# The output gate's low-rank products in three passes of split operands

## The chip, the core and the metric

The kernel runs on one core of a Trainium2 chip. The metric is device time in microseconds of one execution. Five engines work side by side, each through its own list of instructions in order: TensorE (PE in the profile, its weight loads PEld), VectorE (DVE), ScalarE (ACT), GpSimd (POOL) and SyncE (SP). They wait for each other by semaphores. Matmul results land in PSUM, everything else lives in SBUF, and the weights come from memory by DMA.

## The reference

One layer of an encoder trunk, 256 tokens, model width 2048, all in float32. The input is normalised, one combined projection feeds three mixers, their outputs are gated and summed, then an output projection, a norm, and an MLP with squared ReLU. The first mixer is stick-breaking attention, the second forgetting attention, the third an RWKV-7 time mix with 16 heads of 64. The change lies in the third:

```python
r, k, v, wd, ad, gd = _split(z, (RWKV_WIDTH,) * 3 + (DECAY_LORA, AAA_LORA, GATE_LORA))
w_log = -jax.nn.softplus(-(w0 + jnp.tanh(wd) @ w_up)) - 0.5
a = jax.nn.sigmoid(a0 + ad @ a_up)
g = jax.nn.sigmoid(gd) @ g_up
...
y = ((y - mean) * lax.rsqrt(var + RWKV_GN_EPS) * ln_w + ln_b)
y = y + jnp.sum(r_h * k_h * r_k, axis=-1, keepdims=True) * v_h
return y.reshape(b, s, RWKV_WIDTH) * g
```

`g` is the output gate: 160 inner channels (`GATE_LORA`), a sigmoid, and a product with `g_up`, 160 by 1024. The 160 channels are laid out as 128 and 32. The result `y * g` is the operand of the third branch, `y_c @ w_branch_c`.

## The kernel before

**The main stream.** The weights come as one stream of halves of 128 x 1024 floats. `wraw` loads a half on SP's queue, `wsplit` cuts it into a rounded part (`whi`, an ACT copy, line 173) and a rest (`wlo`, a DVE subtraction, line 175); each of `raw`, `whi` and `wlo` has three buffers. The activations are cut the same way: 16 tiles `pk` of 512 columns, 256 of the rounded part and 256 of the rest. A product is then three passes of rounded operands (high times high, high times low, low times high), on type float32r. `unit` (lines 191, 195, 197) gives a tile of channels by tokens; `tok` (lines 220, 235) gives tokens by 512 channels, with 12 matmuls of 512 columns per weight half. In `tok`, the last half runs first for the first 128 tokens and then for the other 128 (line 220). `gate` is one `tok` of eight halves with a tanh as evacuation (line 1017), `branch` one `tok` over a mixer's output (four halves for the third mixer), with two DVE operations as evacuation (lines 1029, 1030).

**The mixers.** All three are one Python generator, `mixers()`, whose steps are emitted between the matmuls of the main stream. `tick(f)` adds 0.88 f to a credit, at most up to 1.5, and takes f from a hold; while the credit is positive and the hold has run out, `step()` emits the next piece, and the piece's own cost, written in its `yield`, is taken from the credit. A yield of `("stage", cost, hold)` sets a hold as well and ends the tick. A yield of `("need", key)` stops until the main stream has produced that tile. `tok` ticks with 0.7, 0.5 and 0.5 per half, with 1.0 twice in the last half; `unit` ticks with 1.0 twice per half. Each `branch` takes 0.6 or 1.2 per 128 tokens from the credit.

TensorE's order is the order of emission, by hand. In this part of the kernel ACT, DVE, POOL and the queues are ordered by the planner, which takes an instruction once its operands and buffers are free, in favour of those emitted earlier.

**The third mixer.** `rwkv_lora` (lines 655 to 663) applies tanh and sigmoid to the low-rank inputs: `xl` for decay and learning rate, which is split into `xs` for rounded products, and `sy` (128 channels of the gate) and `zz` (the gate's other 32 on partitions 0 to 31, copied onto 32 to 63 by line 660), which stay plain fp32. Then `rwkv_half` runs twice, for eight heads each: key norms (L709 to L717), four gate steps (`gates`, with rounded products on line 731 in two row groups), the triangular inverse in the buffer `Ti` (L819 to L867), four chunks of the state (right-hand sides in the buffer `rh`, read by line 885), and at last two blocks of group norm, each for two pairs of heads:

- the gate weights `gq` are loaded by four DMAs on ACT's queue (lines 924, 925), into a buffer of their own, `gup`;
- squares, and their split into `hi`, `lo` (lines 929 to 932), then a stage with cost 0.1 and hold 2.5;
- sums over heads in two passes (lines 100, 101), the gate products in plain fp32 (lines 938 and 941, the latter on 32 partitions, one pair of heads per row group);
- variance, power by Ln and Exp with their table loads (lines 942, 265, 267), a Newton step (272 to 275), scaling, bias, bonus and gate (950 to 953).

After that `cut` (called at each tick) splits the finished `y` into `pk` tiles for the third branch (lines 256, 257).

**The place in the stream.** The second half's blocks fall into the three third-mixer gates, `thc`, which stand ahead of the third branch. After them the line `while not fin[0]: step()` emits at once what is left of the mixer, and the third branch follows; its operands of the last two pairs of heads are used by its fourth weight half.

Of the kernel before, what the change touches and what calls it, by code (L numbers as in the profile page):

```python
# [11 lines left out]
F32 = mybir.dt.float32  # L12
F32R = mybir.dt.float32r
AF = mybir.ActivationFunctionType
ALU = mybir.AluOpType
# [3 lines left out]
T = 256  # L19
# [33 lines left out]
def hybrid_block(ctx, tc, xt, x, gains, params, consts, lora, gup, wst, out):  # L53
    nc = tc.nc
    V, A, G, PE = nc.vector, nc.scalar, nc.gpsimd, nc.tensor
# [10 lines left out]
    def nm(s):  # L66
        uid[0] += 1
        return f"{s}_{uid[0]}"
# [4 lines left out]
    def mps():  # L73
        return pm.tile([128, 512], F32, tag="mps", name=nm("mps"), bufs=4)
# [4 lines left out]
    def tmp(n=T):  # L79
        return tpool.tile([128, T], F32, tag="tmp", name=nm("tmp"), bufs=3)  # L80
# [22 lines left out]
    def P(name, i=0, r=slice(0, 128)):  # L103
        return par[r, PC[name] + i:PC[name] + i + 1]


    done = {}
# [92 lines left out]
    def unit(pks):  # L200

        ps = gps()
        for h in range(2):
            hi, lo = wnext()
            gemm(ps, hi, lo, pks[8 * h:8 * h + 8], h == 0, h == 1, tick)
        return ps
# [40 lines left out]
    def evac(ps, dst):  # L247
        b = tmp()
        ins = A.activation(b, ps[:, T:2 * T], AF.Copy)
        V.tensor_tensor(dst, ps[:, 0:T], b, ALU.add)  # L250
        return ins
# [11 lines left out]
    def power(y, m, t):  # L263

        A.activation(t, m, AF.Ln)
        yield
        A.activation(y, t, AF.Exp, scale=-0.5)
        yield

    def newton(y, m, t):  # L270

        V.tensor_tensor(t, y, y, ALU.mult)
        V.tensor_tensor(t, t, m, ALU.mult)
        V.tensor_scalar(t, t, -0.5, 1.5, ALU.mult, ALU.add)
        V.tensor_tensor(y, y, t, ALU.mult)

    p1 = ExitStack()
    rp = p1.enter_context(tc.tile_pool(name="rp", bufs=1))
# [3 lines left out]
    def g1(w=T):  # L282
        return rp.tile([128, T], F32, tag="g1", name=nm("g1"), bufs=21)


    z = tmp()
# [353 lines left out]
    def shift(ps, i, dst, n=128):  # L640

        b, t = tmp(), tmp()
        zp = rp.tile([128, T + 1], F32, tag="zp", name=nm("zp"), bufs=2)
        G.memset(zp[:, 0:1], 0.0)
        A.activation(b[0:n], ps[0:n, T:2 * T], AF.Copy)
        V.tensor_tensor(t[0:n], ps[0:n, 0:T], b[0:n], ALU.add)
        A.activation(zp[0:n, 1:T + 1], t[0:n], AF.Copy, scale=P("mu", i, slice(0, n)))
        V.scalar_tensor_tensor(dst, t[0:n], omu[0:n, i:i + 1], zp[0:n, 0:T], ALU.mult, ALU.add)
# [3 lines left out]
    def rwkv_lora():  # L652
        yield ("need", "lora")
        xl, sy, zz = done["zx"], done["zy"], done["zz"]
        A.activation(xl[0:64], xl[0:64], AF.Tanh)
        sz = zz[0:32]
        for s in (sy, sz):
            A.activation(s, s, AF.Tanh, scale=0.5)
            V.tensor_scalar(s, s, 0.5, 0.5, ALU.mult, ALU.add)
        A.activation(zz[32:64], sz, AF.Copy)  # L660
        xs = rp.tile([128, 2, T], F32R, name="xs")
        A.activation(xs[:, 0, :], xl, AF.Copy)
        V.tensor_tensor(xs[:, 1, :], xl, xs[:, 0, :].bitcast(F32), ALU.subtract)
        done["xl"], done["sy"], done["sz"] = xs, sy, zz
        yield 1.5

    def pair(tag="AX", bufs=5):
        return rp.tile([128, 2, T], F32R, tag=tag, name=nm("hl"), bufs=bufs)

    def heads(ps, hi, lo):  # L670
        twice(ps, CR("bones"), *(t.rearrange("p a b -> p (a b)") for t in (hi, lo)))

    def rwkv_half(hf):
        PR = range(4 * hf, 4 * hf + 4)
        xl, sy, sz = done["xl"], done["sy"], done["sz"]
# [10 lines left out]
        for i2 in range(2):  # L686
            hi, lo = pair(), pair()
            for i, p in enumerate(PR[2 * i2:2 * i2 + 2]):
                yield ("need", f"k{p}")
                kx[p] = done[f"k{p}"]  # L690
                s = tmp()
# [81 lines left out]
        for i, p in enumerate(PR):  # L773
# [7 lines left out]
            for cc in range(4):  # L781
                for h in range(2):
                    hr = slice(64 * h, 64 * h + 64)
                    PE.matmul(pss[h][:, cc * 128:cc * 128 + 128], At[p][hr, cc, :], Bt[p][hr, cc, :],
                              start=True, stop=True)
# [30 lines left out]
        Ti = rp.tile([64, 32, 32], F32, tag="Ti", name=nm("Ti"), bufs=1)  # L816
# [9 lines left out]
        for s in range(31):  # L826
            n, m = 31 - s, s + 1
# [37 lines left out]
        for c in range(4):  # L865
# [8 lines left out]
            for i, p in enumerate(PR):  # L874
                for h, hc in enumerate(HC):
                    PE.matmul(psr[hc, co[i]], SC[64:128, sls[i][h], 0:64], Xt[p][64:128, c, hc],
                              start=c == 0 and i == 0, stop=True, skip_group_check=True)
# [26 lines left out]
            for i, p in enumerate(PR):  # L904
                for h, hc in enumerate(HC):
                    PE.matmul(psy[hc, co[i]], Xt[p][:, c, hc], SC[:, sls[i][h], 64:128],
                              start=c == 0 and i == 0, stop=True, skip_group_check=True)
            if c < 3:
                for hr in HC:
                    d, n = psp[hr, 0:T].rearrange("p (a b) -> p a b", a=4), Pb[hr, :, hr]  # L910
# [6 lines left out]
            yield ("stage", 1.5, 1.7)  # L917

        for i2 in range(2):
            gq = rp.tile([128, 3, 128], F32, tag="gup", name=nm("gup"), bufs=1)  # L920
            for i in range(2):
                cs = slice(128 * PR[2 * i2 + i], 128 * PR[2 * i2 + i] + 128)
                with tc.issue_after(behind[1].ins):
                    nc.scalar.dma_start(out=gq[:, i, :], in_=gup[0:128, cs])
                    nc.scalar.dma_start(out=gq[32 * i:32 * i + 32, 2, :], in_=gup[128:160, cs])
            B6 = rp.tile([128, 6, T], F32, tag="b6", name=nm("gn"), bufs=1)
            var, ri, sc = B6[:, 0:2, :], B6[:, 2:4, :], B6[:, 4:6, :]
            for i in range(2):
                A.activation(sc[:, i, :], y[PR[2 * i2 + i]], AF.Square)
            hi, lo = pair(), pair()  # L930
            A.activation(hi, sc, AF.Copy)
            V.tensor_tensor(lo, sc, hi.bitcast(F32), ALU.subtract)
            yield ("stage", 0.1, 2.5)
            ps = mps()
            heads(ps, hi, lo)
            psg = [mps(), mps()]
            for i in range(2):
                PE.matmul(psg[i][:, 0:T], gq[:, i, :], sy, start=True, stop=False)
            for i in range(2):
                r = slice(32 * i, 32 * i + 32)  # L940
                PE.matmul(psg[i][:, 0:T], gq[r, 2, :], sz[r], start=False, stop=True)
            A.activation(var, ps.rearrange("p (a b) -> p a b", a=2), AF.Identity, scale=1.0 / 64, bias=cst[:, 1:2])
            yield ("stage", 0.1, 0)
            for _ in power(ri, var, sc):
                yield ("stage", 0.1, 1)
            newton(ri, var, sc)
            yield 2.2
            for i in range(2):
                p = PR[2 * i2 + i]
                V.tensor_tensor(y[p], y[p], ri[:, i, :], ALU.mult)  # L950
                A.activation(y[p], y[p], AF.Identity, scale=P("lnw", p), bias=P("lnb", p))
                V.tensor_tensor(y[p], y[p], bon[p], ALU.add)
                V.tensor_tensor(y[p], psg[i][:, 0:T], y[p], ALU.mult)
                yc[p] = y[p]
                yield 1.1

    def mixers():
        yield from sb_mix()
        yield from fox_mix()
        yield from rwkv_lora()  # L960
        for hf in range(2):
            yield from rwkv_half(hf)
# [4 lines left out]
    def vtok(sb):  # L967
        vs = []
        for tt, ps in enumerate(tok(xpk if sb else upk)):
            v = rp.tile([128, 512], F32, tag="BK", name=nm("vtok"), bufs=8)  # L970
            if sb:
                A.activation(v, ps, AF.Copy, scale=col[:, 4 * tt:4 * tt + 1])
            else:
                A.activation(v, ps, AF.Copy)
            vs.append(v)
        return vs

    for br in ("sb", "fox"):
        for s in ("q", "k"):
            if br == "sb":  # L980
                continue
            lst = []
            for h in range(4):
                ps = unit(upk)
                t = g1()
                evac(ps, t)
                lst.append(t)
            done[br + s] = lst
        done[br + "v"] = vtok(br == "sb")
        done[br] = True  # L990
        for i, nme, n in ((0, "zx", 128), (1, "zy", 128)) if br == "fox" else ((2, "zz", 36),):
            ps = unit(upk)
            z = rp.tile([128, T], F32, tag="tha", name=nme, bufs=1) if i == 0 else \
                rp.tile([64 if n == 36 else n, T], F32, name=nme)
            shift(ps, MU_X + i, z[0:n], n)
            done[nme] = z
    done["lora"] = True
# [180 lines left out]
    for g in range(4):  # L1178
        gs = slice(512 * g, 512 * g + 512)
# [338 lines left out]
    for g in range(4):  # L1518
        gs = slice(512 * g, 512 * g + 512)
# [140 lines left out]
```

## Time and profile before

| | us |
|---|---|
| median of three runs | 1508.16 |
| lowest, highest | 1507.34, 1508.66 |
| the profiled execution's own time | 1509.36 |
| its span | 1507.6 |

The profile gives one execution. A group is a line, an engine, an operation and its tiles, with durations in ns. The chain of waits is followed back from the last instruction; its pieces have start, length, engine, line and count. In a timeline, a row has start, length, engine, line, operation, output and input, and in brackets the idle time before it and what ended it. A plain fp32 product of 256 columns shows as two TensorE records, a float32r product as one. Matmul ends are modelled, so rows of successive matmuls overlap; the distance of their starts is what TensorE spends on them.

### The profile page before, as it was taken

To read this page: it belongs to the slowest core of one execution; us is meant where nothing else is said; L and a number is where in the kernel's file an instruction comes from. 1 tells how busy PE (TensorE), PEld (TensorE's weight loads), DVE (VectorE), ACT (ScalarE), POOL (GpSimd) and SP (SyncE) were. 2 spreads that over 40 slices of the span, in tenths; PEclk is the share of its full clock that TensorE was granted. 3 is DMA by queue.
4 is the path that set the end of the run, shared out by engine and by line. 5 is a ranking of instruction groups with operands and counts; after the bars stand their busy time and mean duration, and the time that the engine had idled before them with its cause. 6 is when DMAs were issued, how large, how long until landed. Compare 5 with 4: busy or idle time off the path is not lost.

```text
span 1507.6 us, 22703 instructions
## 1 busy us (share of the span) xinstructions
PE 1492.0 (99%) x8384; PEld 1254.0 (83%) x8384; DVE 1206.6 (80%) x1673; ACT 939.8 (62%) x1433; POOL 94.5 (6%) x151
## 2 busy tenths in 40 slices
PE   9999999999999999999999999999999999999997
PEld 7888888887788887788888988888888888888886
DVE  7875679895678796476557778998899989999996
ACT  7665677545676445564545766776667666767663
POOL 0021003000001000000000000000000000000000
PEclk9999999999999999999999999999999999999999
DMA  7655454454455465456675768888888888989874
GB/s 263 197 168 184 142 182 154 154 182 163 156 165 177 154 192 186 130 169 196 231 238 159 265 177 254 229 242 273 263 259 258 244 254 248 258 254 258 246 224 152
DMA packets 104687, 312.71 MB, mean 207 GB/s; under 512 B 10240, under 2 KB 12288, under 8 KB 104576
## 3 DMA queue, kind: packets, MB, share of 16 engines
q1 hardware_dynamic: 93968, 279.87, 56.2%
q0 software_dynamic: 8064, 29.36, 10.5%
q10 hardware_dynamic: 2544, 2.03, 0.5%
q8 instruction: 66, 1.08, 0.3%
q14 instruction: 45, 0.37, 0.1%
HBM read 279.77 MB, written 2.10 MB: 187 GB/s over the span
## 4 chain that ended last, share of the span: by engine, by line
PE 89%; DMA 4%; DVE 2%; issue 2%; ACT 2%; POOLq 0%; SPq 0%; DVEq 0%; POOL 0%; ACTq 0%
PE gps L235 27%; PE gps L191 21%; PE gps L195 12%; PE gps L220 7%; PE mps L1378 3%; PE mps L1380 3%; PE mps L1379 3%; DMA raw<-in_wst_dram 2%; PE gps L1380 2%; PE gps L1378 2%; PE gps L1379 2%; DMA raw<-raw 2%; PE gps L197 1%; DVE wlo L175 1%; ACT whi L173 1%
## 5 line engine op out<-in xcount | busy, mean ns | idle before, releaser
L175 DVE TENSOR_TENSOR wlo<-raw,whi 128x1024 fp32r<-128x1024 f32 x576 | 699.0, 1224 | 159.2 <-ACT whi L173 147.3
L173 ACT ACTIVATE whi<-raw 128x1024 fp32r<-128x1024 f32 x576 | 604.1, 1057 | 260.4 <-PE gps L235 76.3
L191 PE MATMUL gps<-pk,whi 128*128 128x512 f32 x1479 | 375.6, 392 | 1.8 <-DVE tmp L1296 1.0
L191 PEld LDWEIGHTS gps<-pk,whi 128*128 128x128 f32 x1479 | 274.2, 188 | 57.9 <-ACT whi L173 2.3
L235 PE MATMUL gps<-whi,pk 128*128 128x512 f32 x1004 | 253.6, 393 | 0.0
L195 PEld LDWEIGHTS gps<-pk,wlo 128*128 128x128 f32 x1582 | 215.6, 190 | 15.6 <-DVE wlo L175 0.7
L195 PE MATMUL gps<-pk,wlo 128*128 128x256 f32 x1582 | 221.1, 283 | 0.1
L235 PEld LDWEIGHTS gps<-whi,pk 128*128 128x128 f32 x1004 | 186.6, 188 | 39.8 <-issue 1.0
L235 PE MATMUL gps<-wlo,pk 128*128 128x512 f32 x502 | 138.2, 393 | 0.1
L235 PEld LDWEIGHTS gps<-wlo,pk 128*128 128x128 f32 x502 | 93.2, 188 | 20.0 <-DVE wlo L175 0.5
L1378 PE MATMUL mps<-whi,fm 128*128 128x512 f32 x224 | 88.8, 396 | 0.8 <-ACT whi L173 0.6
L1295 ACT ACTIVATE tmp<-gps 128x256 f32<-128x256 f32 x64 | 24.6, 384 | 101.4 <-PE gps L197 99.5
L1379 PE MATMUL mps<-whi,fm 128*128 128x512 f32 x224 | 87.8, 392 | 0.0
L1380 PE MATMUL mps<-wlo,fm 128*128 128x512 f32 x224 | 87.6, 391 | 0.0
L1358 POOL DMA_DIRECT2D raw<-raw x56 | 48.8, 872 | 573.1 <-DVE raw L1355 279.5
L1355 DVE TENSOR_TENSOR raw<-raw,raw 128x1024 f32<-128x1024 f32 x56 | 68.5, 1222 | 0.8
L1378 PE MATMUL gps<-whi,fm 128*128 128x512 f32 x168 | 65.9, 392 | 0.0
L1380 PE MATMUL gps<-wlo,fm 128*128 128x512 f32 x168 | 65.9, 392 | 0.0
L1379 PE MATMUL gps<-whi,fm 128*128 128x512 f32 x168 | 65.5, 390 | 0.0
L220 PE MATMUL gps<-whi,pk 128*128 128x512 f32 x224 | 60.8, 393 | 0.0
L1380 PEld LDWEIGHTS mps<-wlo,fm 128*128 128x128 f32 x224 | 42.1, 188 | 9.7 <-DVE wlo L175 0.2
L1378 PEld LDWEIGHTS mps<-whi,fm 128*128 128x128 f32 x224 | 42.4, 189 | 8.9 <-ACT whi L173 2.9
(346 smaller groups left out, 1726.6 us busy)
## 6 DMA issues: line engine op xcount, KB each, us to landing
raw<-in_wst_dram SPq DMA_DIRECT2D x516, 512.0 KB, 4.4
raw<-raw POOLq DMA_DIRECT2D x56, 512.0 KB, 6.8
x<-in_xt_dram SPq DMA_DIRECT2D x8, 256.0 KB, 6.7
x<-in_x_dram SPq DMA_DIRECT2D x8, 256.0 KB, 4.7
raw<-in_wst_dram SPq DMA_DIRECT2D x4, 256.0 KB, 4.9
g<-in_gains_dram SPq DMA_DIRECT2D x4, 256.0 KB, 4.8
pk<-in_gains_dram SPq DMA_DIRECT2D x4, 256.0 KB, 6.9
out_dram<-x SPq DMA_DIRECT2D x4, 256.0 KB, 2.8
```

Source lines behind the costliest of these rows:

```text
L173: A.activation(hi, raw, AF.Copy)
L175: low = lambda: V.tensor_tensor(lo, raw, hi.bitcast(F32), ALU.subtract)
L191: PE.matmul(ps, hi[:, i * 128:i * 128 + 128], pks[i], start=first and i == 0, stop=False)
L195: PE.matmul(ps[:, 0:T], lo[:, i * 128:i * 128 + 128], pks[i][:, 0:T], start=False, stop=False)
L220: PE.matmul(ps[tt], pks[k][:, c:c + 128], w[:, (k - k0) * 512:(k - k0) * 512 + 512], start=k == 0 and part == 0 and w is hl[0], stop=w is ...
L235: PE.matmul(ps[tt], pks[k][:, c:c + 128], w[:, (k - k0) * 512:(k - k0) * 512 + 512], start=k == 0 and part == 0 and w is hl[0], stop=False)
L1295: A.activation(b, ps[:, T:2 * T], AF.Copy)
L1355: V.tensor_tensor(R[d, a], R[d, a], R[d, b], ALU.add)
L1358: G.dma_start(out=R[d, a], in_=R[d, b], accum_op=ALU.add)
L1378: PE.matmul(Q[f], a, w, start=d == d0 and i == 0, stop=False)
L1379: PE.matmul(Q[f], b, w, start=False, stop=False)
L1380: PE.matmul(Q[f], a, wl, start=False, stop=d == dn and i == 1)
```

## The change

`rwkv_lora` splits the sigmoids `sy` and `zz` into a rounded part and a rest, and its cost goes from 1.5 to 2.5. Each group norm block splits its gate weights too, into `gs`, after a new yield of 0.8, and its stage costs 0.8 in place of 0.1. The gate products are three float32r passes (high by high, high by low, low by high) for each former fp32 product; the passes on 32 partitions alternate between the two row groups. `gq` moves from `gup` into the buffer tag `rh`, `gs` goes into `Ti`, and the projected inputs `zy` and `zz` move from tiles of their own into the tags `em` and `kkr`.

```diff
@@ -658,11 +658,17 @@
         A.activation(zz[32:64], sz, AF.Copy)
+        parts = []
+        for s, n in ((sy, 128), (zz, 64)):
+            t = rp.tile([128, 2, T], F32R, name=nm("ss"))[0:n]
+            A.activation(t[:, 0, :], s[0:n], AF.Copy)
+            V.tensor_tensor(t[:, 1, :], s[0:n], t[:, 0, :].bitcast(F32), ALU.subtract)
+            parts.append(t)
         xs = rp.tile([128, 2, T], F32R, name="xs")
         A.activation(xs[:, 0, :], xl, AF.Copy)
         V.tensor_tensor(xs[:, 1, :], xl, xs[:, 0, :].bitcast(F32), ALU.subtract)
-        done["xl"], done["sy"], done["sz"] = xs, sy, zz
-        yield 1.5
+        done["xl"], done["sy"], done["sz"] = xs, *parts
+        yield 2.5
@@ -917,7 +923,8 @@
         for i2 in range(2):
-            gq = rp.tile([128, 3, 128], F32, tag="gup", name=nm("gup"), bufs=1)
+            gq = rp.tile([128, 3, 128], F32, tag="rh", name=nm("gup"), bufs=1)
+            gs = rp.tile([128, 2, 3, 128], F32R, tag="Ti", name=nm("gs"), bufs=1)
@@ -930,15 +937,22 @@
             V.tensor_tensor(lo, sc, hi.bitcast(F32), ALU.subtract)
-            yield ("stage", 0.1, 2.5)
+            yield 0.8
+            for r, c in ((slice(0, 128), slice(0, 2)), (slice(0, 64), slice(2, 3))):
+                A.activation(gs[r, 0, c, :], gq[r, c, :], AF.Copy)
+                V.tensor_tensor(gs[r, 1, c, :], gq[r, c, :], gs[r, 0, c, :].bitcast(F32), ALU.subtract)
+            yield ("stage", 0.8, 2.5)
             ps = mps()
             heads(ps, hi, lo)
             psg = [mps(), mps()]
+            three = ((0, 0), (0, 1), (1, 0))
             for i in range(2):
-                PE.matmul(psg[i][:, 0:T], gq[:, i, :], sy, start=True, stop=False)
-            for i in range(2):
-                r = slice(32 * i, 32 * i + 32)
-                PE.matmul(psg[i][:, 0:T], gq[r, 2, :], sz[r], start=False, stop=True)
+                for a, b in three:
+                    PE.matmul(psg[i][:, 0:T], gs[:, a, i, :], sy[:, b, :], start=a + b == 0, stop=False)
+            for a, b in three:
+                for i in range(2):
+                    r = slice(32 * i, 32 * i + 32)
+                    PE.matmul(psg[i][:, 0:T], gs[r, a, 2, :], sz[r, b, :], start=False, stop=a == 1)
@@ -990,8 +1004,7 @@
-            z = rp.tile([128, T], F32, tag="tha", name=nme, bufs=1) if i == 0 else \
-                rp.tile([64 if n == 36 else n, T], F32, name=nme)
+            z = rp.tile([128, T], F32, tag=("tha", "em", "kkr")[i], name=nme, bufs=1)
```

## The prediction

> **What bounds the kernel now.** I read the page's busy times first, then who TensorE waits for, then the chain of waits around the four places that change.
>
> ```profile
> PE 1492.0 (99%) x8384; PEld 1254.0 (83%) x8384; DVE 1206.6 (80%) x1673; ACT 939.8 (62%) x1433; POOL 94.5 (6%) x151
> PE 89%; DMA 4%; DVE 2%; issue 2%; ACT 2%; POOLq 0%; SPq 0%; DVEq 0%; POOL 0%; ACTq 0%
> ```
>
> TensorE is busy 99% of the span and 89% of the chain. So a change in TensorE's own work, or a wait put into its fixed order, goes straight into the time; work added to DVE or ACT costs only where TensorE then waits for it. The third mixer lies between about 180 and 668 us. There the waits of TensorE's matmuls are this one row, and the stretches (columns: length, then busy time of PE, PEld, DVE, ACT, POOL, then the granted clock) say the same:
>
> ```profile
> PE gps L191 <- ACT whi L173: 0.5, 1, 0.5
> 180.00:250.00 70.00, 69.36 (x418) 60.29 (x417) 55.87 (x94) 52.36 (x99) 8.31 (x19) 1.00 0.53 167
> 420.00:480.00 60.00, 59.94 (x290) 48.82 (x290) 48.73 (x67) 38.37 (x51) 5.04 (x8) 1.00 0.59 184
> 600.00:663.00 63.00, 63.00 (x500) 49.73 (x499) 34.08 (x55) 39.28 (x71) 0.00 (x0) 1.00 0.42 135
> ```
>
> TensorE loses 0.64 us in the first stretch, 0.06 in the second, nothing in the third. DVE is near 80% in the first two.
>
> **The products themselves.** The four group norm blocks (two pairs of heads in each half) hold the changed products; this is how the tile of gate weights and the chain show them:
>
> ```profile
> L938 PE MATMUL mps<-zy,gup x16: 378/379/380, 393.6 to 654.9; 128*128 128x256 f32 x16
> L941 PE MATMUL mps<-zz,gup x16: 374/426/479, 394.6 to 655.5; 32*128 32x256 f32 x16
> 637.74 0.86 PE mps L938 x4
> ...
> 639.24 14.73 PE gps L235 x64
> ...
> 654.43 0.86 PE mps L938 x4
> 655.29 0.63 PE mps L941 x4
> 655.92 4.76 PE gps L235 x20
> 660.68 2.72 PE gps L220 x12
> 663.40 8.16 PE gps L235 x36
> ```
>
> Sixteen records for eight products on each line: a plain fp32 product is two records. A block holds four of line 938 in 0.86 us (0.215 each) and four of line 941 in 0.63. For rounded operands two groups stand as measure, both with 256 columns:
>
> ```profile
> 234.73 0.95 PE gps L195 x8
> ...
> 251.79 0.91 PE mps L731 x12
> ```
>
> Line 195 takes 0.95 / 8 = 0.119 us a pass. Six such passes replace line 938's four records: 0.71 for 0.86, a gain of 0.15. Line 731 is 12 passes that alternate between two row groups, 0.91 / 12 = 0.076 each; six replace line 941's four: 0.46 for 0.63. But part of the 0.91 is the entry into row groups, which stays whole:
>
> ```profile
> PEld mps L941 <- issue: 1.3, 4, 0.3
> ```
>
> That is 0.3 us in front of each block's line 941, where nothing the profile shows is waited for. I take 0.05 gained there and 0.2 a block in all. Bounds for a block: 0.32 gained (0.15 + 0.17, no fixed entry), and 0.16 lost, if the six row group passes cost as much each as line 941's records (0.63 / 4 = 0.157, six are 0.94, 0.31 lost against 0.15 gained).
>
> **The splits.** New in the low-rank preparation: two ACT copies and two DVE subtractions; in each block two of each again. The same shapes stand in the trace as the split of the decay inputs:
>
> ```profile
> L662 ACT ACTIVATE xs<-zx x1: 402/402/402, 169.1 to 169.1; 128x256 fp32r<-128x256 f32 x1
> L663 DVE TENSOR_TENSOR xs<-zx,xs x1: 424/424/424, 171.2 to 171.2; 128x256 fp32r<-128x256 f32 x1
> ```
>
> So ACT gets ten at no more than 0.40, 4 us, and DVE ten at no more than 0.42, 4.2 us, spread over five places. At the blocks the cover is weights split well ahead: the stretch that holds two blocks, 600 to 663, has DVE busy 34 of 63 us, and a hold of 2.5 stands between the splits and the matmuls that use them. In the stretch 180 to 250 the cover is thin. There I put 0.1 us for the preparation's splits, between 0 and 0.85 (the whole of the two subtractions).
>
> **The tiles that move.** The gate weights leave their own buffer for the one that the state's right-hand sides use, so a half's first load can no longer run far ahead; it starts after the last reader of those sides, and its split waits for it.
>
> ```profile
> DMA to landing us min/median/max: 1.7/2.7/5.0
> L885 PE MATMUL mps<-rh,SC x128: 217/218/268, 351.6 to 626.9; 64*64 64x64 f32 x128
> ```
>
> The last reader is at 626.9, the block's products at 637.74: 11 us for a load of 1.7 to 5.0 and two splits. The loads are issued on ACT's queue, where a wait for that release would hold the whi copies behind it; whi has three buffers, so I cost it at 0, and at 1.0 if the cover fails (one whi copy's length). The split gate weights sit in the buffer of the triangular inverse: the second half's LoRA load now waits for the second block's products, some 60 us before it is used. The z tiles in two buffers of the gate step are read out before that step begins: 0.
>
> **What the planner's costs do.** This is the term that decides. Emission of the mixer is metered: a tick of weight f adds 0.88 f of credit (at most 1.5), a step needs positive credit and an expired hold. The change raises the charge by 1.0 in the preparation and 1.5 in each block, 7.0 in all. A gate's stream gives 0.7 + 0.5 + 0.5 per weight half of 12 matmuls and twice 1.0 in the last: 23 ticks. Running the kernel's own rule through with the new charges, the first half runs one tick late, then two after its blocks begin; the second half starts five late and enters its chunk loop seven late, since holds that end with full credit give back only part. Take the last block, with the ticks of the third gate numbered 1 to 23. Before: squares at tick 11, hold 2.5; ticks 12 to 16 give 0.5, 0.7, 0.5, 0.5, 0.7 = 2.9, so its products are placed at tick 16, after 5 x 12 + 4 = 64 matmuls; that is the row of x64. After: squares at tick 17 with credit 0.09; minus 0.8 leaves -0.71; ticks 18 and 19 add 0.44 and 0.62, so the weight splits come at tick 19, and the hold takes 0.5 + 0.5 + 1 + 1, to tick 23. The products then stand behind all 96 matmuls of the gate, and all that follows them (power, Newton, scaling, cut) is emitted at once, ahead of the third branch.
>
> So the last block comes 32 matmuls later in TensorE's order. From the 36 in 8.16 us, a matmul is 0.227, and 32 are 7.26 us. What it has to be in time for, and when its results were ready before (TensorE, then ACT, then DVE):
>
> ```profile
> 654.03 0.40 PE L101 MATMUL mps<-hl,cr 128*128 128x512 f32 x1
> 671.40 1.07 PE L220 MATMUL gps<-whi,pk 128*128 128x512 f32 x4
> ```
> ```profile
> 652.19 1.06 ACT L173 ACTIVATE whi<-raw 128x1024 fp32r<-128x1024 f32 x1 [0.22 <-PE gps L235]
> 654.47 0.69 ACT L942 ACTIVATE gn<-mps,cst 128x512 f32<-128x512 f32 x1 [1.21 <-PE mps L101]
> ...
> 658.41 0.63 ACT L267 ACTIVATE gn<-gn 128x512 f32<-128x512 f32 x1
> 658.95 1.99 ACT L173 ACTIVATE whi<-raw 128x1024 fp32r<-128x1024 f32 x2
> ```
> ```profile
> 659.07 0.69 DVE L272 TENSOR_TENSOR gn<-gn 128x512 f32<-128x512 f32 x1 [4.56 <-ACT gn L267]
> ...
> 660.87 1.22 DVE L175 TENSOR_TENSOR wlo<-raw,whi 128x1024 fp32r<-128x1024 f32 x1
> 662.01 0.69 DVE L275 TENSOR_TENSOR gn<-gn 128x512 f32<-128x512 f32 x1
> ...
> 663.41 1.22 DVE L175 TENSOR_TENSOR wlo<-raw,whi 128x1024 fp32r<-128x1024 f32 x1
> 664.54 0.76 DVE L952 TENSOR_TENSOR g<-g,g 128x256 f32<-128x256 f32 x2
> ...
> 666.90 0.43 DVE L257 TENSOR_TENSOR pk<-g,pk 128x256 fp32r<-128x256 f32 x1 [0.36 <-ACT pk L256]
> ```
>
> The sums end at 654.43, the last operand of the third branch is there at 667.33: 12.9 us. TensorE wants it two matmuls after 671.40, at 671.85. The slack is 4.52, the move 7.26: short by 2.74 us, in which TensorE has nothing else in its order. Two wlo subtractions stood inside the 12.9; without both it would be some 1.8 shorter (the second partly hid behind ACT's scaling). After the move the branch's first three weight halves can be split before the sums end, since each whi buffer comes free as a half's high products end (the copy at 652.19 shows it), so I expect one wlo inside, 0.8 less: a wait of 1.9 us. Bounds: 0.9 (no wlo inside) and 3.8 (two, and one whi copy of 1.06 in front on ACT). The block's own gain of 0.2 disappears in this wait, so only three blocks count.
>
> Sum: -3 x 0.2 + 1.9 + 0.1 = +1.4 us. The profiled execution took 1509.36 (span 1507.6 and 1.76 around it), which would become 1510.8. It lay 1.2 above the median of the runs, 1508.16, on which I put the forecast: 1509.6.
>
> **The rivals.**
> *Not slower: the last block still arrives in time.* The slack of 4.52 us is 20 matmuls. If the block is placed no more than those 20 later, or its tail is shorter by the missing 2.7, four blocks of gain remain: 1508.16 - 0.8 = 1507.4. For it: holds swallow most of the 7.0 charged. Against it: the count above ends 12 matmuls beyond that.
> *Deeper wait.* ACT takes a whi copy or the gate's tanh ahead of the block's chain and both wlo stay inside: 3.8 - 0.6 + 0.1 = +3.3, 1511.5. For it: at 658.95 two copies queue right at the chain. Against: they came after it.
> *DVE becomes the bound in the crowded places.* The key norm steps near 213 to 230 and 441 to 460 shift by one and five ticks against the weights; a wait of one wlo (1.22) at each adds 2.4 to the forecast: 1512.0. For it: 0.64 us lost there already. Against: 0.06 in the second place.
> *The clock falls after the wait.* If TensorE is granted half its clock for the first weight half of the branch, 12 matmuls of 0.227 take 2.7 us more: 1512.3. In the rows above the clock is 1.00 with no wait over 0.5 us, so they can't decide. The Trainium skill, "TensorE: Matmul & The Clock Gate", section "Why this matters for your kernels", warns of gaps over about 3 us between bursts, after which the clock drops to half; by that rule a wait of 1.9 us is too short, and one of 3.8 would not be.
> *The passes gain nothing.* Then -0.6 becomes 0 and the time 1510.2, inside the forecast.
>
> **How the numbers follow.** A measurement here tells about 0.2% from no change, 3.0 us: 1505.1 to 1511.2. Forecast, with a wait between 0.9 and 3.5 us: 0.53, own range 1508.4 to 1511.1. In time: 0.15. Deeper wait: 0.17. DVE bound: 0.08. Clock: 0.03. Something unseen that gains over 3 us: 0.04. Within: 0.53 + 0.15 = 0.68; slower: 0.17 + 0.08 + 0.03 = 0.28; faster: 0.04. The range runs from the rival in time to the DVE rival, 1507.4 to 1512.0, and leaves out the clock and the unseen gain.
>
> **What would show it.** In the profile after: TensorE's block near 0.5 + 0.7 us in place of 1.49; the last block's sums directly in front of the third branch's matmuls; and a TensorE wait of about 2 us on a DVE split of the branch operands, in the branch's first pass, where there was none. If that wait is missing the time lies below 1508.2; if it is over 3 us, or TensorE waits for wlo in the first half of the mixer, the time lies above the forecast.

## The result and the profile after

The changed kernel takes 1520.0 us (median of four runs, 1518.9 to 1520.6), the kernel before 1508.1. The ratio is 1.0078, with a 95% interval of 1.0066 to 1.0089: 11.9 us slower. The profiled execution took 1518.93 us with a span of 1517.1; that span is 9.5 us longer than before. The medians differ by 2.4 us more than the two profiled executions do, since this one is the shortest of its four and that of the kernel before lay 1.2 above its median.

First the page of the changed kernel, busy times and then the chain's shares by engine:

```profile
PE 1494.1 (98%) x8400; PEld 1255.3 (83%) x8400; DVE 1211.9 (80%) x1683; ACT 942.9 (62%) x1443; POOL 97.2 (6%) x151
PE 89%; DVE 5%; DMA 2%; ACT 2%; issue 2%; SPq 0%; DVEq 0%; POOLq 0%; POOL 0%; ACTq 0%
```

DVE rose from 2% to 5% of the chain (DMA fell from 4% to 2%), and DVE is not 3% busier: it got 5 us of work. So some of its work now seems to stand in TensorE's way. What TensorE's matmuls wait for between 180 and 720 us (total, times, longest), where there was one row of 0.5 us before:

```profile
PE gps L220 <- ACT pk L256: 4.9, 1, 4.9
PE gps L195 <- DVE wlo L175: 1.6, 2, 1.3
PE gps L235 <- DVE wlo L175: 1.2, 1, 1.2
PE gps L220 <- DVE wlo L175: 0.6, 1, 0.6
PE gps L235 <- ACT whi L173: 0.2, 1, 0.2
```

The first row is the third branch's operand, the last block's result: TensorE waits first for the ACT copy of it, where the prediction named the DVE split. The chain around it, start and length:

```profile
640.70 5.44 PE gps L235 x24
...
646.59 0.71 PE mps L951 x6
647.30 0.55 PE mps L955 x4
647.85 13.84 PE gps L235 x60
661.69 2.72 PE gps L220 x12
664.41 0.23 PE mps L100
...
678.97 0.42 ACT pk L256
679.39 0.04 issue
679.44 0.65 PE gps L220
680.09 0.03 issue
680.12 4.14 PE gps L220 x11
684.26 8.18 PE gps L235 x36
```

The products of a block take 0.71 + 0.55 = 1.26 us, 0.23 less than the 1.49 before. The block before the last stands after 24 matmuls of the third gate, and from there it is 60 + 12 to the last block's sums at 664.41: the last one stands behind all 96, as counted in the prediction. And the matmuls behind the wait are slow: from 679.44 to 684.26 the branch's last half takes 4.8 us, where 12 matmuls took 2.72 before. Two stretches, the first ahead of the end of the wait and the second behind it, show one reason, the granted clock being the third number from the end:

```profile
676.00:679.40 3.40, 0.00 (x0) 0.00 (x0) 3.00 (x7) 1.51 (x3) 0.00 (x0) 1.00 0.85 249
679.40:684.00 4.60, 4.53 (x12) 3.32 (x13) 2.40 (x5) 0.53 (x2) 0.00 (x0) 0.63 0.12 45
```

The other reason is that DVE's part of the operands comes later than ACT's; the weight load of the second matmul waits for it:

```profile
680.11 0.93 PEld L220 LDWEIGHTS gps<-whi,pk 128*128 128x128 f32 x3 [0.49 <-DVE pk L257]
```

So the profiled execution adds up: 4.9 of wait, 4.8 - 2.7 = 2.1 of a slower last half (1.4 of it the clock and 0.7 the later operands, by the run with the filled wait below), and 1.6 + 1.2 + 0.6 + 0.2 = 3.6 of other waits against 0.5 before, 3.1; together 10.1. Four blocks give back 4 x 0.23 = 0.9. That is 9.2 of the 9.5.

Why the wait was so long is in the block's chain on ACT and DVE (the rows between are left out):

```profile
664.47 0.39 PE L101 MATMUL mps<-hl,cr 128*128 128x512 f32 x1
...
665.48 0.59 ACT L1030 ACTIVATE th<-gps 128x512 f32<-128x512 f32 x1
...
667.92 1.04 ACT L173 ACTIVATE whi<-raw 128x1024 fp32r<-128x1024 f32 x1
...
671.89 1.23 DVE L175 TENSOR_TENSOR wlo<-raw,whi 128x1024 fp32r<-128x1024 f32 x1 [0.26 <-ACT whi L173]
...
673.64 1.22 DVE L175 TENSOR_TENSOR wlo<-raw,whi 128x1024 fp32r<-128x1024 f32 x1
...
675.83 1.22 DVE L175 TENSOR_TENSOR wlo<-raw,whi 128x1024 fp32r<-128x1024 f32 x1
...
680.21 0.42 DVE L257 TENSOR_TENSOR pk<-g,pk 128x256 fp32r<-128x256 f32 x1 [0.15 <-ACT pk L256]
```

From the end of the sums (664.86) to the last operand (680.63) it is 15.8 us; before it was 12.9 and I had counted on 12.1. The gate's tanh and one whi copy stand inside it on ACT, and three wlo between the steps on DVE instead of two. One tanh, one whi copy and one wlo are 0.59 + 1.04 + 1.23 = 2.9 us, which is the growth.

### The profile page after: what moved, and what is told of

The parts are those of the page before. It is cut to its first block, busy times and chain, and to the rows that moved or that the text cites. A ratio compares the mean times of both kernels' runs of the same rounds, so it can differ in the third digit from the quotient of the medians.

```text
span 1517.1 us, 22764 instructions
## 1 busy us (share of the span) xinstructions
PE 1494.1 (98%) x8400; PEld 1255.3 (83%) x8400; DVE 1211.9 (80%) x1683; ACT 942.9 (62%) x1443; POOL 97.2 (6%) x151
## 4 chain that ended last, share of the span: by engine, by line
PE 89%; DVE 5%; DMA 2%; ACT 2%; issue 2%; SPq 0%; DVEq 0%; POOLq 0%; POOL 0%; ACTq 0%
PE gps L235 25%; PE gps L191 21%; PE gps L195 11%; PE gps L220 7%; PE mps L1391 3%; PE mps L1393 3%; PE mps L1392 3%; PE gps L1393 2%; PE gps L1391 2%; PE gps L1392 2%; DVE wlo L175 2%; DMA raw<-in_wst_dram 2%; PE gps L197 1%; ACT whi L173 1%; PE mps L790 1%
## 5 line engine op out<-in xcount | busy, mean ns | idle before, releaser
L235 PEld LDWEIGHTS gps<-whi,pk 128*128 128x128 f32 x1004 | 186.7, 188 | 40.2 <-ACT whi L173 0.7
L220 PEld LDWEIGHTS gps<-whi,pk 128*128 128x128 f32 x224 | 41.7, 191 | 14.7 <-ACT pk L256 5.3
```

What stands on the lines that cost most here:

```text
L220: PE.matmul(ps[tt], pks[k][:, c:c + 128], w[:, (k - k0) * 512:(k - k0) * 512 + 512], start=k == 0 and part == 0 and w is hl[0], stop=w is ...
L235: PE.matmul(ps[tt], pks[k][:, c:c + 128], w[:, (k - k0) * 512:(k - k0) * 512 + 512], start=k == 0 and part == 0 and w is hl[0], stop=False)
```

## The experiments

The first theory was that the new costs move the last block and that the move alone makes the loss (the place). Its rival was that the added splits and the shared buffers make weights late wherever the block stands. All ratios are against runs of the kernel before on the same chip.

**Without the new yield.**

```diff
-            yield 0.8
             for r, c in ((slice(0, 128), slice(0, 2)), (slice(0, 64), slice(2, 3))):
```

> The changed kernel without its new yield of 0.8 (the stage's cost 0.8 and the preparation's 2.5 stay). Run through the rule of the ticks, the last block then stands after 64 matmuls of the third gate again, as before the change, and not after 96. Theory A (the place): the wait of 4.9 us on the branch operands goes, and so does the lower clock behind it (12 matmuls in 4.5 us in place of 2.7): 6.7 us less than the changed kernel's 1520.0, and some of the 2.9 us of earlier waits: 1510.4 to 1513.3. Theory B (the added splits and shared buffers make the weights' low parts late, wherever the block stands): the wait goes but the chain stays long, 1516 or more.

It took 1510.4 us, 1.0019 (1.0010 to 1.0029): 9.6 less than the changed kernel by the medians. In its chain the last block stands after 64 matmuls again, and the wait on the operands is gone (chain, the row between the second half's two blocks):

```profile
642.32 14.75 PE gps L235 x64
```

Left are the waits for wlo:

```profile
PE gps L195 <- DVE wlo L175: 1.5, 2, 1.3
PE gps L235 <- DVE wlo L175: 1.3, 1, 1.3
```

One line that adds no instruction carries most of the loss. The waits that stay are the rest of the question.

**All old costs, with the three passes, splits and buffers.**

```diff
-        yield 2.5
+        yield 1.5
...
-            yield 0.8
...
-            yield ("stage", 0.8, 2.5)
+            yield ("stage", 0.1, 2.5)
```

> The changed kernel with all its costs as before (no new yield, stage 0.1, preparation 1.5); three passes, splits and buffers stay. Theory A (the place): every step of the mixer stands where it stood before, so what is left is the gain in the products, up to 0.8 us, and whatever the splits cost: 1507.4 to 1509. Theory B (splits and buffers): the 2.9 us of waits for wlo in the first three quarters of the mixer stay, 1510.5 or more.

It took 1507.9 us, 1.0002 (0.9993 to 1.0011). The waits are back to the single row of the kernel before, and the last block is in its place (chain; the two rows above are the block before it):

```profile
636.96 0.71 PE mps L950 x6
637.67 0.55 PE mps L954 x4
638.22 14.74 PE gps L235 x64
```

The splits and the shared buffers therefore cost nothing that can be measured, and the second theory falls. The gain of 0.9 us in the products cannot be told from no change either.

**The new costs alone, on the kernel before.** The same three yields, set to the new values in the kernel before.

> The kernel before with the new costs alone (preparation 2.5, a yield of 0.8 and a stage of 0.8 in each block); products in plain fp32, no splits, buffers as before. Theory A (the place): as slow as the changed kernel, 1517 to 1521, with a wait of 3 to 6 us on the branch operands in the third branch. Theory B (splits and buffers): near the kernel before, 1507.5 to 1510.

It took 1519.6 us, 1.0079 (1.0066 to 1.0091), with a wait of 4.6 us on the branch operands. The whole loss appears with no changed product in the kernel.

**The yield alone, on the kernel before.**

```diff
-            yield ("stage", 0.1, 2.5)
+            yield 0.8
+            yield ("stage", 0.1, 2.5)
```

> The kernel before with only the new yield of 0.8 in each block; stage 0.1 and preparation 1.5 as before. By the rule of the ticks the last block then stands after 90 matmuls of the third gate (64 before, 96 in the changed kernel). If the yield's place is the cause, TensorE waits 3 to 5 us on the branch operands, the clock falls behind it, and the time is 1514 to 1517, without the early waits for wlo. If the amount charged counts and not the yield, the time stays under 1510.

It took 1514.4 us, 1.0045 (1.0031 to 1.0059), 6.1 us more by the medians. Its chain shows the block between the gate's last two groups of six, its wait, and the clock behind it:

```profile
658.47 1.36 PE gps L220 x6
659.83 0.23 PE mps L100
...
661.79 1.59 PE gps L220 x6
```
```profile
PE gps L220 <- ACT pk L256: 3.7, 1, 3.7
```
```profile
676.00:680.00 4.00, 4.00 (x12) 3.12 (x11) 1.38 (x2) 0.44 (x1) 0.00 (x0) 0.57 0.23 92
```

There are no early waits for wlo.

**The preparation's cost alone, on the kernel before.**

```diff
-        yield 1.5
+        yield 2.5
```

> The kernel before with one number changed: the preparation's cost 2.5 in place of 1.5, so that the first half's key norms come one tick later; the last block stays after 64 matmuls of the third gate. If the changed kernel's early waits for wlo (1.6 us near 215 to 232, 1.2 near 342) come from this one tick, both are here, and the time is that of the kernel without the new yield, about 1510.4. If they come from the preparation's four split instructions, there is neither, and the time is 1508.1.

It took 1511.3 us, 1.0018 (1.0009 to 1.0027). The key norms come one tick later, and both early waits are there:

```profile
PE gps L195 <- DVE wlo L175: 1.6, 2, 1.3
PE gps L235 <- DVE wlo L175: 1.2, 1, 1.2
```

So they come from that one tick and not from the four split instructions of the preparation: these are absent here, and with them and the old costs the waits were absent. The waits end at about 238, 244 and 343 us. Which instruction displaces which wlo there was not taken apart.

**The stage's cost alone, on the kernel before.**

```diff
-            yield ("stage", 0.1, 2.5)
+            yield ("stage", 0.8, 2.5)
```

> The kernel before with the blocks' stage cost at 0.8 in place of 0.1 and nothing else. By the rule of the ticks every block stays where it was, since the hold of 2.5 behind it lets the credit fill up to its cap either way. If placement is all that costs act through, the time is that of the kernel before, 1507.8 to 1508.8. If a charge costs time by its amount, 1509.5 or more.

It took 1508.8 us, 1.0000 (0.9991 to 1.0009). The amount charged there does nothing, and in the chain the last block stands after 64 matmuls as before. With the yield's 6.1 and the preparation's 2.9, 9.0 of the 11.5 that the three costs make together are accounted for; the rest comes with both at once (a later place of the block, and a wait of 4.6 in place of 3.7).

**Twelve matmuls later.** Only the last block's hold is raised, on the kernel before, to probe the slack.

```diff
-            yield ("stage", 0.1, 2.5)
+            yield ("stage", 0.1, 4.2 if hf and i2 else 2.5)
```

> The kernel before with the hold of the last block alone raised from 2.5 to 4.2: its products come after 76 matmuls of the third gate, 12 more than before, 2.7 us. If the slack is the 4.5 us that the trace of before shows, TensorE doesn't wait and the time is 1507.9 to 1508.5. If the planner gives the room away to other work as soon as the block moves, there is a wait on the branch operands of 0.5 to 2 us, and the time is 1508.8 to 1511.

It took 1508.6 us, 1.0002 (0.9993 to 1.0011), and TensorE has no new wait. The block is moved by 2.7 us and is in time (chain, then the last operands on DVE):

```profile
639.22 17.45 PE gps L235 x76
```
```profile
669.25 0.75 DVE L257 TENSOR_TENSOR pk<-g,pk 128x256 fp32r<-128x256 f32 x2
```

The operands are ready at 670.0; the branch first uses the last pairs at 671.4. The slack read from the trace holds for such a move.

**The next stream's splits behind the chain.** In the changed kernel, the first two halves of the stream after the branch are split only behind the last cut, on both engines.

```diff
+            if keep and n in keep[1]:
+                with tc.issue_after(keep[0][0].ins):
+                    A.activation(hi, raw, AF.Copy)
+                with tc.issue_after(keep[0][1].ins):
+                    return V.tensor_tensor(lo, raw, hi.bitcast(F32), ALU.subtract)
...
+        keep.extend((last[0], (gc + 20, gc + 21)))
```

> The changed kernel with the splits of the next gate's or branch's first two weight halves issued behind the last cut of the third mixer, on ACT and on DVE. In the changed kernel two wlo subtractions of 1.22 us that the third branch doesn't need stood inside the block's chain. If they are what made the chain 15.8 us long in place of 12.9, it shrinks by about 2.2, the wait goes from 4.9 to about 2.7, and with the lower clock the time falls by 2.2 to 3.9: 1516.1 to 1517.8. If the length comes from elsewhere, the wait stays over 4 us and the time near 1520.

It took 1517.7 us, 1.0057 (1.0045 to 1.0070), 2.4 less than the changed kernel by the medians. The wait is shorter by 2.0, and the clock behind it still falls (its line numbers are six higher):

```profile
PE gps L226 <- ACT pk L262: 2.9, 1, 2.9
```
```profile
680.00:684.00 4.00, 4.00 (x13) 3.20 (x13) 2.35 (x4) 2.31 (x3) 0.00 (x0) 0.68 0.16 50
```

The chain from the sums to the last operand is 13.8 us here in place of 15.8. So early splits of two halves that nobody needed yet cost it 2.0 us. The edit moves their whi copies as well, but in the changed kernel ACT had 2.7 us idle behind them, so the two wlo are what counts. The tanh and one whi copy are still inside.

**TensorE kept busy in the wait.** The changed kernel with 18 extra matmuls ahead of the branch's last half.

```diff
+                    for _ in range(fill[0]):
+                        PE.matmul(d, pks[0][:, 0:128], pks[0], start=True, stop=True)
```

> The changed kernel with 18 more matmuls of 512 columns (4.1 us) on operands that are there, into a PSUM tile that nobody reads, placed right ahead of the third branch's fourth weight half, where TensorE waits 4.9 us. They change no result. If the slow matmuls after the wait are a clock that falls with the idle time, the wait shrinks to about 0.8 us, the clock stays at 1.00 and the time falls by 1.5 to 1.9 us: 1518.1 to 1518.5. If they are something else (operands or weights that are late), the time stays at 1520.

It took 1518.2 us, 1.0065 (1.0051 to 1.0079), 1.8 less than without the extra work by the medians. The two intervals overlap, so the trace has to carry the reading. The wait is down to what the 18 don't fill, and the clock stays:

```profile
676.60 4.24 PE L229 MATMUL mps<-pk 128*128 128x512 f32 x18
681.69 0.50 PE L220 MATMUL gps<-whi,pk 128*128 128x512 f32 x1 [0.85 <-ACT pk L261]
...
685.11 1.98 PE L240 MATMUL gps<-whi,pk 128*128 128x512 f32 x8
```
```profile
680.00:684.00 4.00, 2.98 (x12) 1.75 (x11) 2.42 (x7) 1.60 (x4) 0.00 (x0) 1.00 0.45 146
```

This separates the parts of the slow half: at full clock it takes 685.11 - 681.69 = 3.4 us, in the changed kernel 4.8, and before the change 2.7. So about 1.4 us belong to the clock and 0.7 to the operands from DVE; no wait for weights shows there.

**A cheaper preparation.** The kernel with all old costs, and the preparation at 0.5.

```diff
-        yield 1.5
+        yield 0.5
```

> The changed kernel with the old costs, and the preparation's cost at 0.5 in place of 1.5, so that the first half's key norms come one tick earlier than in the kernel before. If a tick later costs 2.9 us because it crowds two places, a tick earlier may free the 0.5 us that TensorE still loses near 214: 1507.0 to 1507.6, and the version would beat both kernels. If the kernel before stands at a place where either direction crowds, 1508 to 1511.

It took 1509.0 us, 1.0002 (0.9993 to 1.0010): no gain in this direction. In its trace the one wait of 0.5 us, which stands at 229 us and not near 214, is replaced by one of 0.9 for a wlo at 231. No version here is measurably faster than the kernel before.

## Why the prediction was wrong

The direction and the main place were right, the size was not: 1.4 us were forecast, 11.9 came, and the range ended at 1512.0.

In the profiled execution the terms differ from the forecast by +3.0 (the wait), +2.1 (the slow half behind it), +3.0 (the first half) and -0.3 (the products); with the 1.4 forecast that is the 9.2 added up above.

- **The products.** Forecast 0.2 gained per block, measured 0.23. Right, and too small to matter.
- **The place of the last block.** Forecast behind all 96 matmuls, found there. But "7.0 in all" was the wrong account of it. The stage's part costs nothing, because the hold behind it refills the credit. What moves the block is that the new yield ends a step: with credit at 0.09 it turns negative, and the second piece has to wait for ticks. This is the kernel's rule worked through; that the yield moves the block is shown, but a yield with no charge was not run.
- **The wait.** This step failed: "I expect one wlo inside, 0.8 less: a wait of 1.9 us". The chain had no fewer but more foreign work inside, 15.8 us in place of 12.1, and the wait was 4.9, above the upper bound of 3.8. The rival of the deeper wait, with 0.17, had the mechanism (the tanh or a whi copy ahead on ACT, both wlo inside), but not the third wlo. I took the order on DVE from when buffers come free. The planner also put splits in for the next stream, which nobody needed; moving two of them out gave 2.0 back. A smaller slip goes the other way: by the order of `tok` the last operand is wanted three matmuls after 671.40 and not two, so the slack was 0.2 us larger than 4.52.
- **The clock.** The rival with 0.03 came true: 1.4 us by the traces, where 2.7 had been priced. I had thought a wait of 1.9 us too short for it. That went by the rule of about 3 us in the Trainium skill ("TensorE: Matmul & The Clock Gate", section "Why this matters for your kernels"). The falls after 4.9 and 3.7 us agree with that rule; but the runs show a fall at its edge, after 2.9 us, and well below it, after 1.2 to 1.9 in four executions (last section), so the measurement decides against relying on it.
- **The first half.** The 0.1 us "for the preparation's splits" was mis-attributed and too small. The splits cost nothing; the one tick by which the whole first half is late costs 2.9. The DVE rival, with 0.08, had the mechanism and nearly the size, 2.4 for two waits, but its places only in part: the first waits stand just behind the key norms, at 238 and 244 us, and the other at 343; near 441 to 460 there is only one of 0.2, for a whi copy.
- **Costed at nothing** and so found, by the run with all old costs: the moved buffers, the later loads, the splits in the blocks.

The three separate misses had the same sign, and the rivals priced each of them alone; together they left the range.

## What to carry to other kernels

In a kernel whose work is metered into a main stream, a changed cost or a new yield is a change of the order, and has to be priced as such: find what is emitted last, where it lands, and how much slack its consumer has. Here the slack read from the trace held for a move of 2.7 us and not for one of 7.3; past it, the work that filled the gap was not the work one would choose, so such a shortfall should be given a wide upper bound. A wait on the bounding engine costs more than its length if its clock falls with it.

## What the runs showed of the hardware

The clock can fall after a much shorter wait than I had thought. In the kernel without the new yield, TensorE waited 1.34 us at about 341 us, and its next eight matmuls took 3.38 us in place of 1.98; the stretch shows the clock:

```profile
342.30 0.73 PE L235 MATMUL gps<-wlo,pk 128*128 128x512 f32 x2 [1.34 <-DVE wlo L175]
...
344.21 3.38 PE L235 MATMUL gps<-whi,pk 128*128 128x512 f32 x8
```
```profile
344.00:348.00 4.00, 4.00 (x12) 3.14 (x11) 1.74 (x2) 2.43 (x5) 0.00 (x0) 0.57 0.87 314
```

In the profiled execution of the changed kernel, with a wait of 1.19 us at the same place, the clock stays full:

```profile
344.00:348.00 4.00, 4.00 (x31) 3.28 (x19) 1.80 (x2) 1.89 (x4) 0.00 (x0) 1.00 0.82 287
```

The kernel with the preparation's cost alone waited 1.19 us there too, and has full clock. But in three more traces the clock fell there: in the kernel before with the new costs alone after 1.17 us, with the next stream's splits behind the chain after 1.17, and with the wait filled after 1.92. The next eight matmuls took 3.52, 3.50 and 3.06 us. Of the first, the wait; then the stretch of all three:

```profile
342.58 0.73 PE L235 MATMUL gps<-wlo,pk 128*128 128x512 f32 x2 [1.17 <-DVE wlo L175]
```
```profile
344.00:348.00 4.00, 4.00 (x11) 3.14 (x12) 1.18 (x2) 1.43 (x2) 0.00 (x0) 0.57 0.88 301
344.00:348.00 4.00, 4.00 (x41) 3.16 (x29) 1.76 (x2) 1.72 (x3) 0.00 (x0) 0.58 0.87 275
344.00:348.00 4.00, 4.00 (x73) 3.23 (x73) 1.81 (x3) 1.29 (x2) 0.00 (x0) 0.58 0.84 256
```

So the length of the wait alone does not decide: 1.17 us had a fall behind it and 1.19 had none. What decides, where the wait falls in some window for instance, these runs don't tell. Such a fall costs about 1.4 us on these eight matmuls (3.38 - 1.98).

Executions without a trace have only their mean granted clock on record. Without the new yield it is 0.996 in the two longest (1513.4 and 1514.3 us, the second being the profiled one) and 0.997 or 0.998 in the seven others, down to 1509.0. In the changed kernel it is 0.997 in the profiled execution and 0.995 in the three longer ones. A fall near 344 us in some executions fits both, and would be part of the 2.4 us between the medians and the profiled executions; it is not shown for them. A difference of 1 to 2 us between two versions that wait there can therefore not be read from their times alone, which is why the 2.0 and 1.4 us above are taken from traces.
